# Implicit-filter taps computed with time on the partitions, their norm and the bias term summed by accumulating DMAs, and the convolution's output rows formed one quarter later

## The chip, the cores and the metric

The kernel runs on one core of a Trainium2 chip. The metric is the device time of one execution in microseconds, the median of several runs; one further execution was recorded by the profiler. Everything is float32; products of large matrices are made as three matmuls of a high and a low part (hi x hi, hi x lo, lo x hi).

## The reference

One encoder layer on 512 tokens of width 2048. An RMS-normalised input is projected; two branches run on it, a Hyena branch (gated long convolution, 1024 channels) and grouped-query attention; they are gated, merged and projected, and a SwiGLU feed-forward network follows. The change touches the Hyena branch alone:

```python
def implicit_filter(L, w1, b1, w2, b2, w3, b3, w4, freq):
    ...                                  # z: 33 features of each of the 512 positions
    h = jnp.sin(fr * (z @ w1 + b1))
    h = jnp.sin(fr * (h @ w2 + b2))
    h = jnp.sin(fr * (h @ w3 + b3))
    h = h @ w4                           # (512, 2048): a forward and a backward filter per channel
    ...
    decay = jnp.exp(-t[:, None] * deltas[None, :])
    h_fwd = h[:, :HYENA_W] * decay
    h_bwd = h[:, HYENA_W:] * decay
    k = jnp.concatenate([h_fwd, jnp.zeros((1, HYENA_W), f32), h_bwd[:0:-1]], axis=0)
    return k / jnp.sum(jnp.abs(k), axis=0, keepdims=True)

    x0, x1, hv = jnp.split(u_h, HYENA_ORDER + 1, axis=-1)     # after a 3-tap convolution
    z = hv * x1
    z = bidir_fft_conv(z, filt) + hy_bias * z
    y_h = z * x0
```

So the taps are made by a small network from the positions, damped, divided by the sum of their absolute values, and convolved with z through a transform of 1024 points; a bias times z is added.

## The kernel before

The 1024 Hyena channels are handled in four quarters q of 256 channels, each two tiles c of 128 channels. The main program (the loop over q near line 602) multiplies the 16 input tiles xg by weight blocks of 128 x 128 (`group`: three matmuls per block), makes x1, hv and x0 with `short_conv`, and then z and its even and odd parts zf. Weights come in tiles of 1024 columns: a load on SP's queue into one of two buffers, a cast on ScalarE (wh) and a subtraction on VectorE (wl), each with three buffers.

The filter work is woven into this stream. Generators stand in one queue (`side`); after every weight block `step()` counts one step, and when the number that a generator yielded has passed, its next part is emitted. The order of TensorE is exactly that of emission; the other engines' orders are made by a scheduler with priorities, and stay in order on the chip. The queue holds `mlp_gen` (the three sine layers, once), `taps_gen(0)`, a pause, `filter_gen(0)`, and then for each q `conv_gen(q)`, which contains `taps_gen(q + 1)`, and `filter_gen(q + 1)`.

- `taps_gen(q)` multiplies the last layer's output (hh, hl: 64 hidden units twice on the partitions, 512 positions along the row) by w4: channels on the partitions, time along the row (fp). VectorE multiplies by the decay (dec), giving fd and bd; ScalarE sums the absolute values along the row (scr), VectorE makes 1/norm (rn), adds norm times bias into tap zero, and folds the two halves into hs and hd.
- `filter_gen(q)` turns hs and hd by 16 transposes on TensorE (ktp), so that time is on the partitions, twists them (kt, with priority), splits them into high and low parts (k..h, k..l), and after TURN_WAIT steps transforms them (kp). The spectrum (G, then K) is written to a DRAM tile kd by POOL.
- `conv_gen(q)` transposes and transforms zf (ztp, up), loads the spectrum in two halves fb (kc, POOL's queue), multiplies (cu, cv, Y), and after Y_WAIT steps transforms back (ab); ab times rn gives abs, whose sums and differences are y, and y times x0 is yh.

PSUM has eight banks in one rotation; the tag tmp has five buffers of 128 x 512, the tag wk seven. After the last quarter the key/value projection (kv) runs, `flush()` emits what is left of the queue, and the memory of this stage is released to attention. The q, attention, gate and feed-forward stages that follow are not changed.

Of the kernel before, what the change touches and what calls it, by code (L numbers as in the profile page):

```python
# [40 lines left out]
RS_STEP = 8  # L41
TURN_WAIT = 8, 8, 10, 11
Y_WAIT = 11, 13, 11, 15
# [74 lines left out]

def layer_kernel(tc, wpk, xT, par, flt, zemb, w4, decT, tb2, rope, qkg, out):
    nc = tc.nc  # L120
# [189 lines left out]
    def mlp_gen():  # L310
# [15 lines left out]
        for l in range(3):  # L326
            csl = slice(l * P, (l + 1) * P)
            nk, nh = (P, 64) if l else (66, 33)
            hp = ps_tile(f"hp{l}")
            mm(hp, wh[:nk, csl], st[:nk], True, False)  # L330
            mm(hp, wl[:nh, csl], st[:nh], False, True)
            a = tmp(f"ha{l}")
            nn = tmp(f"hn{l}")
            nc.vector.tensor_scalar(a, hp, fl[:, 256 + l:257 + l], fl[:, 259:260], ALU.add, ALU.mult)
            nc.vector.tensor_scalar(nn, a, float(np.float32(1 / (2 * math.pi))), MAGIC, ALU.mult, ALU.add)
            nc.vector.tensor_scalar(nn, nn, MAGIC, None, ALU.subtract)
            for c in (C1, C2, C3):
                nc.vector.scalar_tensor_tensor(a, nn, -c, a, ALU.mult, ALU.add)
            nc.vector.tensor_scalar(a, a, PI32, -PI32, ALU.min, ALU.max)
            if l < 2:  # L340
                st = tpool.tile([P, S], F32R, tag="tmp", bufs=5, name=f"hs{l}")
                nc.scalar.activation(st, a, AF.Sin)
                casts["sin", l] = nc.scalar.activation(a[64:], a[64:], AF.Sin).ins
                nc.gpsimd.tensor_tensor(st[64:], a[64:], st[64:].bitcast(F32), ALU.subtract)
            else:
                nc.scalar.activation(a, a, AF.Sin)
                hh, hl = cw("hh", [P, S], "hh", dt=F32R), cw("hl", [P, S], "hl", dt=F32R)
                nc.scalar.copy(hh, a)
                nc.vector.tensor_tensor(hl, a, hh.bitcast(F32), ALU.subtract)
                mlp["h"] = hh, hl  # L350
            yield MLP_WAITS[l + 1]
            if l == 2:
                w4_parts(0)
                yield 6

    filt, kd, folded = {}, {}, {}
    w4t = {}
# [6 lines left out]
    def w4_parts(q):  # L364
# [5 lines left out]
        w4t[q] = w4s  # L370

    def taps_gen(q):

        w4s = w4t.pop(q)
        rn, hs_l, hd_l = [], [], []
        for c in range(2):
            dec = cw(f"dec{q}{c}", [P, S], "dec", 1)
            nc.scalar.dma_start(dec, decT[2 * q + c])
            fd = work(f"fd{q}{c}")
            bd = cw(f"bd{q}{c}", [P, S + 1], "bd", 1)  # L380
            for half, dst in ((0, fd), (1, bd[:, :S])):
                fp = ps_tile(f"fp{q}{c}{half}")
                csl = slice(half * 256 + c * P, half * 256 + (c + 1) * P)
                mm(fp, w4s[:, csl], mlp["h"][0], True, False)
                mm(fp, w4s[:, csl], mlp["h"][1], False, True)
                nc.vector.tensor_tensor(dst, fp, dec, ALU.mult)
                yield 2
            nc.vector.memset(bd[:, S:S + 1], 0.0)
            n2 = cw(f"n2{q}{c}", [P, 2], "n2", 3)
            scr = tmp(f"scr{q}{c}")  # L390
            nc.scalar.activation(scr, fd, AF.Abs, accum_out=n2[:, 0:1])
            nc.scalar.activation(scr, bd[:, 1:], AF.Abs, accum_out=n2[:, 1:2])
            r = cw(f"rn{q}{c}", [P, 1], "rn", 4)
            nc.vector.tensor_tensor(r, n2[:, 0:1], n2[:, 1:2], ALU.add)
            nc.vector.scalar_tensor_tensor(fd[:, :1], r, pcol("hyb", 2 * q + c), fd[:, :1], ALU.mult, ALU.add)
            nc.vector.tensor_scalar(r, r, 256.0, None, ALU.mult)
            nc.vector.reciprocal(r, r)
            rn.append(r)

            hs, hd = work(f"hs{q}{c}"), work(f"hd{q}{c}")  # L400
            ahead = fd.rearrange("p (m n) -> p n m", n=2)
            back = bd[:, 1:].rearrange("p (m n) -> p n m", n=2)[:, ::-1]
            for h, op in ((hs, ALU.add), (hd, ALU.subtract)):
                h = h.rearrange("p (n m) -> p n m", n=2)
                nc.vector.tensor_tensor(h[:, :, :P], ahead[:, :, :P], back[:, :, :P], op)
                nc.vector.tensor_tensor(h[:, :, P:][:, :, ::-1], ahead[:, :, P:], back[:, :, P:], op)
            hs_l.append(hs)
            hd_l.append(hd)
        folded[q] = rn, hs_l, hd_l

    def filter_gen(q):
        rn, hs_l, hd_l = folded.pop(q)
        if q + 1 < NQ:
            w4_load(q + 1)
        yield 3
        taps = []
        for i, src in enumerate((hs_l, hd_l)):
            tps = [ps_tile(f"ktp{q}{i}{j}") for j in range(2)]
            for j, tp in enumerate(tps):
                for n in range(4):  # L420
                    o = n // 2 * 256 + j * P
                    transpose(tp[:, n * P:(n + 1) * P], src[n % 2][:, o:o + P])
            with tc.high_priority():
# [6 lines left out]
        if q + 1 < NQ:  # L430
            w4_parts(q + 1)
        yield TURN_WAIT[q]

# [12 lines left out]
        for fb in range(2):  # L446
# [15 lines left out]
            yield 2  # L462
        filt[q] = rn

    zst, x0st, yh = {}, {}, [None] * HT

    def conv_gen(q):

        rn = filt[q]
        while q not in zst or side["n"] < zst[q][2]:  # L470
            yield 1
        zl, zf_l, _ = zst[q]
        zT = []
# [7 lines left out]
        ys = {}  # L481
        for fb in range(2):
            kc = []
            for ph in range(2):
# [9 lines left out]
            for ph in range(2):  # L494
# [9 lines left out]
                ys[ph, fb] = split(r3, y, "r", "r", 16, 16, f"Yt{q}{fb}{ph}")  # L504
                yield 5
        if q + 1 < NQ:
            yield from taps_gen(q + 1)
        yield Y_WAIT[q]
        abs_ = [work(f"abs{2 * q + c}") for c in range(2)]
        for ph in range(2):  # L510
            ab = [ps_tile(f"ab{q}{ph}{c}") for c in range(2)]
            for fb in range(2):
                yhi, ylo = ys[ph, fb]
                a = fb * 256
                for low in range(2):
                    for c in range(2):
                        for i in range(2):
                            csl = slice(i * 256 + c * P, i * 256 + (c + 1) * P)
                            o = ab[c][:, i * 256:(i + 1) * 256]
                            if low:  # L520
                                mm(o[:, :P], ylo[:, csl], part(i, 0, a, a + P), False, fb == 1 and i == 1, skip_group_check=True)
                            else:
                                both = CS[i].rearrange("p (h t) -> p h t", h=2)[:, :, a:a + P]
                                mm(o, yhi[:, csl], both, fb == 0 and i == 0, False, skip_group_check=True)
            yield 4
            for c in range(2):
                low = tmp(f"abl{q}{ph}{c}")[:, :256].rearrange("p (i t) -> p i t", i=2)
                src = ab[c].rearrange("p (i h t) -> p i h t", i=2, h=2)
                nc.scalar.activation(low, src[:, :, 1], AF.Copy, scale=rn[c])
                dst = abs_[c].rearrange("p (i s t) -> p i s t", i=2, s=2)[:, :, ph]  # L530
                nc.vector.scalar_tensor_tensor(dst, src[:, :, 0], rn[c], low, ALU.mult, ALU.add)
        yield 1
        for c in range(2):
            ct = 2 * q + c
# [4 lines left out]
            nc.vector.tensor_tensor(down[:, :, ::-1], a, b, ALU.subtract)  # L539
            while ct not in x0st:  # L540
                yield 1
            yh[ct] = x0st[ct]
            nc.vector.tensor_tensor(yh[ct], yh[ct], y, ALU.mult)


    xps = [ps_tile(f"px{i}") for i in range(XW)]
    xg, acc1 = [], work("acc1")
# [54 lines left out]
    for q in range(NQ):  # L602
        zl, zf_l = [], []
        for c in range(2):
# [10 lines left out]
            hv = short_conv(p2, 16 + ct, f"hv{ct}", cw(f"hvo{ct}", [P, S], "sc", 3))  # L615
            z = cw(f"z{ct}", [P, S], "z", 3)
            nc.vector.tensor_tensor(z, hv, x1, ALU.mult)
            zf = cw(f"zf{ct}", [P, S], "sc", 3)
            after, ahead = (z[:, h * 256:(h + 1) * 256].rearrange("p (t s) -> p s t", s=2) for h in (1, 0))
            for i, op in enumerate((ALU.add, ALU.subtract)):  # L620
                nc.vector.tensor_tensor(zf[:, i * 256:(i + 1) * 256].rearrange("p (s t) -> p s t", s=2),
                                        after, ahead[:, :, ::-1], op)
            zl.append(z)
            zf_l.append(zf)
# [791 lines left out]
def _constants():  # L1416
# [22 lines left out]
    ang = (f4(2.0 * math.pi) * pos / f4(S))[:, None] * fb[None, :]  # L1439
    zemb = two_part(np.ascontiguousarray(np.concatenate([t[:, None], np.cos(ang), -np.sin(ang)], axis=-1).T, dtype=f4)).reshape(66, S)  # L1440
    lo_d, hi_d = math.log(1e-2) / 1.5, math.log(1e-2) / 0.3
    deltas = np.abs(np.linspace(lo_d, hi_d, HW, dtype=f4))
    dec = np.exp(-t[:, None] * deltas[None, :]).astype(f4)
    decT = dec.T.reshape(HT, P, S)

# [3 lines left out]
    for half, pp in ((0, tok // 64), (1, tok % 64)):  # L1449
# [3 lines left out]
        for j, v in enumerate((np.concatenate([c, c], 1), np.concatenate([-s, s], 1))):  # L1453
            rope[:, j, :, b:b + 64] = v.reshape(NTB, P, 64).transpose(1, 0, 2)
    return tb2, cosw, sinw, cosa, sina, zemb, decT, rope


def _arrays(inp):
    f4 = np.float32
    a = {k: np.asarray(v)[0] for k, v in inp.items()}  # L1460
    assert all(v.dtype == f4 for v in a.values())
    tb2, cosw, sinw, cosa, sina, zemb, decT, rope = _constants()

# [43 lines left out]
    xT = a["x"].T.reshape(KT, P, S)  # L1507
    arr = dict(wpk=wpk, xT=xT, par=par, flt=flt, zemb=zemb, w4=w4, decT=decT, tb2=tb2, rope=rope, qkg=qkg)
    return {k: np.ascontiguousarray(v, dtype=f4) for k, v in arr.items()}
# [15 lines left out]
```

## Time and profile before

| | us |
|---|---|
| median of 3 runs | 2494.44 (2492.99 to 2495.07) |
| the profiled execution | 2493.58 |
| its span in the profile | 2491.8 |

TensorE (PE) is busy in all of the span, VectorE (DVE) in 84%, ScalarE (ACT) in 48%, GpSimd (POOL) in 7%. The granted clock of TensorE is full throughout. In the rows of the profile that follow, a timeline row reads: start, busy time, engine, line, operation, result <- inputs, shapes, count, and in brackets the idle time before it and what ended it; a row of waits reads: who, for whom, total, times, longest; a row of stretches reads: stretch and length, then busy us and instruction count of PE, PEld (weight loads), DVE, ACT and POOL, the clock, the DMA engines' share and GB/s. Names like wl or kt are the program's tiles.

### The profile page before, as it was taken

To read this page: it belongs to the slowest core of one execution; us is meant where nothing else is said; L and a number is where in the kernel's file an instruction comes from. 1 tells how busy PE (TensorE), PEld (TensorE's weight loads), DVE (VectorE), ACT (ScalarE), POOL (GpSimd) and SP (SyncE) were. 2 spreads that over 40 slices of the span, in tenths; PEclk is the share of its full clock that TensorE was granted. 3 is DMA by queue.
4 is the path that set the end of the run, shared out by engine and by line. 5 is a ranking of instruction groups with operands and counts; after the bars stand their busy time and mean duration, and the time that the engine had idled before them with its cause. 6 is when DMAs were issued, how large, how long until landed. Compare 5 with 4: busy or idle time off the path is not lost.

```text
span 2491.8 us, 34447 instructions
## 1 busy us (share of the span) xinstructions
PE 2485.5 (100%) x13114; PEld 2140.8 (86%) x13114; DVE 2089.3 (84%) x2972; ACT 1191.4 (48%) x1778; POOL 185.0 (7%) x297
## 2 busy tenths in 40 slices
PE   9999999999999999999999999999999999999999
PEld 7888888888888888888888888888888888888888
DVE  8899986764589999555999989999999988998888
ACT  6444334654554455443544444444444455445443
POOL 0000113020000000000000000000000002001111
PEclk9999999999999999999999999999999999999999
DMA  6434443233554444644333333333333348557754
GB/s 216 132 123 131 140 144 113 70 102 119 185 177 157 148 141 152 194 163 136 121 125 117 127 117 120 127 120 127 118 119 125 121 144 221 146 146 187 193 152 110
DMA packets 113571, 350.48 MB, mean 141 GB/s; under 512 B 13987, under 2 KB 15267, under 8 KB 113181
## 3 DMA queue, kind: packets, MB, share of 16 engines
q1 hardware_dynamic: 70128, 248.02, 30.2%
q0 software_dynamic: 22832, 63.19, 9.6%
q10 hardware_dynamic: 20445, 37.07, 4.9%
q8 instruction: 103, 1.69, 0.3%
q14 instruction: 63, 0.52, 0.1%
HBM read 297.63 MB, written 54.26 MB: 141 GB/s over the span
## 4 chain that ended last, share of the span: by engine, by line
PE 96%; DVE 2%; DMA 1%; issue 0%; ACT 0%; ACTq 0%; SPq 0%; DVEq 0%; POOLq 0%
PE fx L137 19%; PE fy L137 10%; PE b L137 7%; PE o L137 7%; PE gx L137 7%; PE px L137 6%; PE d L137 5%; PE fz L137 5%; PE dx L137 4%; PE q L137 4%; PE ex L137 3%; PE gy L137 3%; PE phv L137 2%; PE ey L137 2%; PE dy L137 2%; PE kv L137 2%
## 5 line engine op out<-in xcount | busy, mean ns | idle before, releaser
L195 DVE TENSOR_TENSOR wl<-wr,wh 128x1024 fp32r<-128x1024 f32 (+1 forms) x168 | 201.2, 1198 | 110.8 <-ACT wh L194 110.6
L194 ACT CAST wh<-wr 128x1024 fp32r<-128x1024 f32 (+1 forms) x168 | 173.3, 1032 | 236.6 <-PE o L137 67.1
L919 ACT CAST fwhs<-fs 128x1024 fp32r<-128x1024 f32 x176 | 184.8, 1050 | 88.7 <-PE fz L137 73.6
L921 DVE TENSOR_TENSOR fwls<-fs,fwhs 128x1024 fp32r<-128x1024 f32 x176 | 214.3, 1218 | 4.3 <-ACT fwhs L919 4.2
L919 ACT CAST fwha<-fa 128x1024 fp32r<-128x1024 f32 x132 | 139.0, 1054 | 149.4 <-PE fx L137 83.4
L137 PE MATMUL px<-xh,wh 128*128 128x512 f32 x576 | 179.4, 393 | 0.4 <-ACT xh L559 0.3
L137 PE MATMUL fy<-fX,fwhs 128*128 128x512 f32 x704 | 175.4, 391 | 0.0
L137 PE MATMUL fx<-fX,fwhs 128*128 128x512 f32 x704 | 175.2, 391 | 0.0
L137 PE MATMUL fx<-fX,fwha 128*128 128x512 f32 x704 | 171.8, 391 | 0.0
L921 DVE TENSOR_TENSOR fwla<-fa,fwha 128x1024 fp32r<-128x1024 f32 x132 | 161.3, 1222 | 10.0 <-ACT fwha L919 9.9
L137 PE MATMUL o<-ms,wh 128*128 128x512 f32 x512 | 157.7, 389 | 0.0
L137 PEld LDWEIGHTS fx<-fX,fwha 128*128 128x128 f32 x704 | 129.3, 188 | 25.0
L137 PEld LDWEIGHTS fx<-fX,fwhs 128*128 128x128 f32 x704 | 129.2, 188 | 25.1
L137 PEld LDWEIGHTS fy<-fX,fwhs 128*128 128x128 f32 x704 | 129.2, 188 | 24.9
L137 PEld LDWEIGHTS px<-xh,wh 128*128 128x128 f32 x576 | 106.7, 188 | 23.3 <-issue 0.7
L137 PE MATMUL d<-act,wh 128*128 128x512 f32 x384 | 118.2, 389 | 0.0
L137 PEld LDWEIGHTS o<-ms,wh 128*128 128x128 f32 x512 | 96.0, 188 | 19.8
L137 PE MATMUL px<-xh,wl 128*128 128x512 f32 x288 | 112.5, 391 | 0.0
L912 DVE TENSOR_TENSOR fs<-fa,fa 128x1024 f32<-128x1024 f32 x88 | 107.0, 1217 | 1.7 <-PE o L137 1.0
L912 DVE TENSOR_TENSOR fs<-fs,fa 128x1024 f32<-128x1024 f32 x88 | 107.2, 1218 | 0.9 <-PE o L137 0.2
L137 PE MATMUL o<-ms,wl 128*128 128x512 f32 x256 | 99.6, 389 | 0.0
L137 PE MATMUL fy<-fX,fwls 128*128 128x256 f32 x704 | 98.7, 283 | 0.2 <-DVE fwls L921 0.2
(979 smaller groups left out, 5883.0 us busy)
## 6 DMA issues: line engine op xcount, KB each, us to landing
fa<-wpk SPq DMA_DIRECT2D x176, 512.0 KB, 3.6
wr<-wpk SPq DMA_DIRECT2D x162, 512.0 KB, 3.5
ga<-wpk SPq DMA_DIRECT2D x60, 512.0 KB, 3.7
da<-wpk SPq DMA_DIRECT2D x32, 512.0 KB, 3.7
ea<-wpk SPq DMA_DIRECT2D x32, 512.0 KB, 4.4
actd<-c POOLq DMA_DIRECT2D x41, 256.0 KB, 4.2
actr<-actd ACTq DMA_DIRECT2D x41, 256.0 KB, 5.1
x2d<-dt POOLq DMA_DIRECT2D x32, 256.0 KB, 5.7
```

The costliest lines, as they stand in the source:

```text
L137: tc.keep_in_program_order(nc.tensor.matmul(out, lhsT=lhsT, rhs=rhs, start=start, stop=stop, **kw))
L194: casts[i] = nc.scalar.copy(st["hi"][:, c], st["raw"][:, c]).ins
L195: nc.vector.tensor_tensor(st["lo"][:, c], st["raw"][:, c], st["hi"][:, c].bitcast(F32), ALU.subtract)
L912: raws["sum"] = nc.vector.tensor_tensor(t, a, b, ALU.add).ins
L919: raws["wh"] = nc.scalar.copy(hi, w).ins
L921: raws["wl"] = nc.vector.tensor_tensor(lo, w, hi.bitcast(F32), ALU.subtract).ins
```

## The change

The features (zemb) are put into another order on the host, all even positions first, so that 128 columns of hh, taken from an offset, are just the positions that one transformed row block needs. In `taps_gen` hh and hl now stand as the stationary operand and w4 moves: fp comes out with time on the partitions and 256 channels along the row for each of two shifts, and the transposes in `filter_gen` are gone. hh and hl get two more columns, and the decay table (decP) is laid out anew, with a zero where the missing tap lies.

The sum over time now runs across partitions. The absolute values of the four tiles of a quarter (fa) are written to one DRAM tile by POOL's queue, the last three with addition in the DMA; `norm_load` brings the sum back on ScalarE's queue and adds its two halves on POOL, and `norm_taps` sums over partitions with two one-column matmuls and makes 1/norm. The bias no longer goes into tap zero: half of bias times zf is written to DRAM (zh, zd), and added to abs by a DMA with addition into SBUF; in the last quarter it is loaded (zr) and added on VectorE. The part that makes y and yh becomes `y_rows`, which for the first three quarters is emitted in the next quarter's `filter_gen`, ahead of TURN_WAIT. Buffers: two for dec instead of one, two for z instead of three, none for bd. TURN_WAIT of the last quarter goes from 11 to 10.

```diff
-TURN_WAIT = 8, 8, 10, 11
+TURN_WAIT = 8, 8, 10, 10
...
-                hh, hl = cw("hh", [P, S], "hh", dt=F32R), cw("hl", [P, S], "hl", dt=F32R)
-                nc.scalar.copy(hh, a)
-                nc.vector.tensor_tensor(hl, a, hh.bitcast(F32), ALU.subtract)
+                hh, hl = (cw(n, [P, S + 2], n, dt=F32R) for n in ("hh", "hl"))
+                for o, src in ((slice(0, 385), a[:, :385]), (slice(386, 513), a[:, 385:]),
+                               (slice(385, 514, P), a[:, P:P + 1].to_broadcast([P, 2]))):
+                    nc.scalar.copy(hh[:, o], src)
+                    nc.vector.tensor_tensor(hl[:, o], src, hh[:, o].bitcast(F32), ALU.subtract)
...
+    TAPS = ((0, 129), (386, 257)), ((1, 129), (385, 257))
+    norms, rns, sums = {}, {}, {}
     def taps_gen(q):
+        folded[q] = []
+        for j in range(2):
+            fb = []
+            for b in range(2):
+                dec = cw(f"dec{q}{j}{b}", [P, S], "dec", 2)
+                nc.scalar.dma_start(dec, decP[4 * q + 2 * j + b])
+                fp = ps_tile(f"fp{q}{j}{b}")
+                for n in range(2):
+                    a = TAPS[b][j][n]
+                    for i in range(2):
+                        mm(fp[:, n * 256:(n + 1) * 256], mlp["h"][i][:, a:a + P], w4s[:, b * 256:(b + 1) * 256],
+                           n == 0 and i == 0, n == 1 and i == 1, skip_group_check=True)
+                f = work(f"f{q}{j}{b}")
+                nc.vector.tensor_tensor(f, fp, dec, ALU.mult)
+                t = tmp(f"fa{q}{j}{b}")
+                nc.scalar.activation(t, f, AF.Abs)
+                if j + b:
+                    nc.gpsimd.dma_start(norms[q], t, accum_op=ALU.add)
+                else:
+                    norms[q] = dpool.tile([P, S], F32, tag=f"nd{q}", bufs=1, name=f"nd{q}")
+                    nc.gpsimd.dma_start(norms[q], t)
+                fb.append(f)
+                if not b:
+                    yield 2
+            f, b = fb
+            hs = work(f"hs{q}{j}")
+            nc.vector.tensor_tensor(hs, f, b, ALU.add)
+            nc.vector.tensor_tensor(f, f, b, ALU.subtract)
+            folded[q].append((hs, f))
+            yield 2
+
+    def norm_load(q):
+        t = tmp(f"na{q}")
+        nc.scalar.dma_start(t, norms[q])
+        norms[q] = cw(f"fo{q}", [P, 256], "fo", 1)
+        nc.gpsimd.tensor_tensor(norms[q], t[:, :256], t[:, 256:], ALU.add)
+
+    def norm_taps(q):
+        acc = norms.pop(q)
+        nr = ps_tile(f"nr{q}")
+        for c in range(2):
+            mm(nr[:, c:c + 1], acc[:, c * P:(c + 1) * P], pcol("one"), True, True)
+        r = cw(f"rn{q}", [P, 2], "rn", 2)
+        nc.vector.tensor_scalar(r, nr[:, :2], 256.0, None, ALU.mult)
+        nc.vector.reciprocal(r, r)
+        rns[q] = [r[:, c:c + 1] for c in range(2)]
...
     def filter_gen(q):
-        for i, src in enumerate((hs_l, hd_l)):
-            tps = [ps_tile(f"ktp{q}{i}{j}") for j in range(2)]
-            for j, tp in enumerate(tps):
-                for n in range(4):
-                    o = n // 2 * 256 + j * P
-                    transpose(tp[:, n * P:(n + 1) * P], src[n % 2][:, o:o + P])
+        for i, tps in enumerate(zip(*folded.pop(q))):
...
         if q + 1 < NQ:
             w4_parts(q + 1)
+        if q:
+            y_rows(q - 1, sums.pop(q - 1))
         yield TURN_WAIT[q]
...
     def conv_gen(q):
         for fb in range(2):
+            if fb:
+                norm_load(q)
...
+        norm_taps(q)
         if q + 1 < NQ:
             yield from taps_gen(q + 1)
         yield Y_WAIT[q]
...
+            if ph and q == NQ - 1:
+                zr = [tmp(f"zr{c}") for c in range(2)]
+                for c in range(2):
+                    nc.scalar.dma_start(zr[c], zd[c])
             yield 4
+            rn = rns[q]
...
+        if q < NQ - 1:
+            for c in range(2):
+                nc.gpsimd.dma_start(abs_[c], zd[c], accum_op=ALU.add)
+            yield 1
+            sums[q] = abs_
+            return
         yield 1
+        for c in range(2):
+            nc.vector.tensor_tensor(abs_[c], abs_[c], zr[c], ALU.add)
+        y_rows(q, abs_)
+
+    def y_rows(q, abs_):
...
-            while ct not in x0st:
-                yield 1
             yh[ct] = x0st[ct]
...
+    hybh = cw("hybh", [P, HT], "hybh")
+    nc.vector.tensor_scalar(hybh, prm[:, PC["hyb"]:PC["hyb"] + HT], 0.5, None, ALU.mult)
...
-            z = cw(f"z{ct}", [P, S], "z", 3)
+            z = cw(f"z{ct}", [P, S], "z", 2)
...
-            zl.append(z)
+            zl.append(dpool.tile([P, S], F32, tag=f"zd{ct}", bufs=1, name=f"zd{ct}"))
+            zh = tmp(f"zh{ct}")
+            nc.scalar.activation(zh, zf, AF.Copy, scale=hybh[:, ct:ct + 1])
+            nc.gpsimd.dma_start(zl[c], zh)
```

More of the change, by code (lines that the diff above doesn't have):

```diff
@@ L116, in weight_blocks, with layer_kernel @@
     return out
-def layer_kernel(tc, wpk, xT, par, flt, zemb, w4, decT, tb2, rope, qkg, out):
+def layer_kernel(tc, wpk, xT, par, flt, zemb, w4, decP, tb2, rope, qkg, out):
     nc = tc.nc
@@ L354, in mlp_gen @@
                 yield 6
-    filt, kd, folded = {}, {}, {}
+    kd, folded = {}, {}
     w4t = {}
@@ L370, in w4_parts @@
         w4t[q] = w4s
+    TAPS = ((0, 129), (386, 257)), ((1, 129), (385, 257))
+    norms, rns, sums = {}, {}, {}
     def taps_gen(q):
         w4s = w4t.pop(q)
-        rn, hs_l, hd_l = [], [], []
-        for c in range(2):
[L377 to L408, printed above, removed]
@@ L409, in taps_gen @@
-        folded[q] = rn, hs_l, hd_l
+        folded[q] = []
[28 more added lines that the diff above has]
+            yield 2
@@ L411, in filter_gen @@
     def filter_gen(q):
-        rn, hs_l, hd_l = folded.pop(q)
         if q + 1 < NQ:
@@ L462, in filter_gen @@
             yield 2
-        filt[q] = rn
     zst, x0st, yh = {}, {}, [None] * HT
     def conv_gen(q):
-        rn = filt[q]
         while q not in zst or side["n"] < zst[q][2]:
             yield 1
-        zl, zf_l, _ = zst[q]
+        zd, zf_l, _ = zst[q]
         zT = []
@@ L1439, in _constants @@
     ang = (f4(2.0 * math.pi) * pos / f4(S))[:, None] * fb[None, :]
-    zemb = two_part(np.ascontiguousarray(np.concatenate([t[:, None], np.cos(ang), -np.sin(ang)], axis=-1).T, dtype=f4)).reshape(66, S)
+    zemb = two_part(np.ascontiguousarray(np.concatenate([t[:, None], np.cos(ang), -np.sin(ang)], axis=-1).T, dtype=f4))
+    order = np.concatenate([i[:257:2], i[1:256:2], i[511:256:-2], i[510:257:-2]])
+    zemb = zemb.reshape(66, S)[:, order]
     lo_d, hi_d = math.log(1e-2) / 1.5, math.log(1e-2) / 0.3
@@ L1443, in _constants @@
     dec = np.exp(-t[:, None] * deltas[None, :]).astype(f4)
-    decT = dec.T.reshape(HT, P, S)
+    p = i[:P]
+    n = np.arange(2)[:, None]
+    at = np.stack([[2 * p + n, 2 * p + 2 - n], [510 - 2 * p + n, 512 - 2 * p - n]])
+    decP = np.concatenate([dec, np.zeros((1, HW), f4)])[at].reshape(4, 2, P, NQ, 256)
+    decP = decP.transpose(3, 0, 2, 1, 4).reshape(4 * NQ, P, S)
     inv = np.power(f4(10000.0), -np.arange(0, 64, 2, dtype=f4) / f4(64)).astype(f4)
@@ L1454, in _constants @@
             rope[:, j, :, b:b + 64] = v.reshape(NTB, P, 64).transpose(1, 0, 2)
-    return tb2, cosw, sinw, cosa, sina, zemb, decT, rope
+    return tb2, cosw, sinw, cosa, sina, zemb, decP, rope
 def _arrays(inp):
@@ L1461, in _arrays @@
     assert all(v.dtype == f4 for v in a.values())
-    tb2, cosw, sinw, cosa, sina, zemb, decT, rope = _constants()
+    tb2, cosw, sinw, cosa, sina, zemb, decP, rope = _constants()
     blocks = weight_blocks()
@@ L1507, in _arrays @@
     xT = a["x"].T.reshape(KT, P, S)
-    arr = dict(wpk=wpk, xT=xT, par=par, flt=flt, zemb=zemb, w4=w4, decT=decT, tb2=tb2, rope=rope, qkg=qkg)
+    arr = dict(wpk=wpk, xT=xT, par=par, flt=flt, zemb=zemb, w4=w4, decP=decP, tb2=tb2, rope=rope, qkg=qkg)
     return {k: np.ascontiguousarray(v, dtype=f4) for k, v in arr.items()}
```

## The prediction

> **What bounds the kernel now.** I read the page's first lines, then who waited for whom on TensorE, then the busy time by stretches, then TensorE's own timeline in the filter stage (roughly 44 to 372 us, where all the changed code runs).
>
> ```profile
> span 2491.8 us, 34447 instructions
> PE 2485.5 (100%) x13114; PEld 2140.8 (86%) x13114; DVE 2089.3 (84%) x2972; ACT 1191.4 (48%) x1778; POOL 185.0 (7%) x297
> ```
>
> ```profile
> PE warm L137 <- DVE wones L252: 1.1, 1, 1.1
> PE kp L137 <- DVE k121l L216: 0.5, 1, 0.5
> PE px L137 <- ACT xh L559: 0.3, 1, 0.3
> PE fy L137 <- DVE fwls L921: 0.2, 1, 0.2
> ```
>
> ```profile
> 200.00:260.00 60.00, 59.52 (x289) 49.61 (x288) 58.60 (x98) 29.59 (x47) 3.13 (x6) 1.00 0.37 115
> ```
>
> TensorE waits about 2 us in the whole program. "Busy" alone proves little, since matmul ends are modelled, but the four waits are the complete list, and the timeline below shows matmuls starting at a constant pitch. So the time is a sum of TensorE pitches; taking work off another engine earns nothing, and anything that makes TensorE wait costs in full. In the third row VectorE (58.60 of 60 us, the third pair) is almost as full: the second bound, close behind.
>
> The profiled execution took 2493.58 us (span 2491.8); the median of the runs is 2494.44, 0.86 higher. I work the change in us against the profiled execution and add it to the median.
>
> **Part 1: the tap transposes leave TensorE.** Eight blocks of eight 128x128 transposes (ktp) go.
>
> ```profile
> 88.38 0.39 PE L137 MATMUL px<-xh,wl 128*128 128x512 f32 x1
> 88.61 0.62 PE L137 MATMUL phv<-xh,wh 128*128 128x512 f32 x2
> 89.06 0.39 PE L137 MATMUL phv<-xh,wl 128*128 128x512 f32 x1
> 89.29 1.03 PE L140 MATMUL ktp<-ident,hs 128*128 128x128 f32 x8
> ...
> 90.86 0.39 PE L137 MATMUL phv<-xh,wh 128*128 128x512 f32 x1
> ```
>
> One weight block is three matmuls, 0.68 us from wl to wl (88.38 to 89.06), a pitch of 0.227. From 88.61 to 90.86 stand two such triples and one transpose block: 2.25 - 1.36 = 0.89 us, with its bubble behind it. Eight blocks: **-7.1 us**.
>
> **Part 2: the tap matmuls turn around.** Before, each of 16 filter tiles had two 512-column matmuls; now each has four of 256 columns, with four weight loads.
>
> ```profile
> 132.97 0.61 PE L137 MATMUL px<-xh,wh 128*128 128x512 f32 x2
> 133.65 0.39 PE L137 MATMUL fp<-hh,w4s 128*128 128x512 f32 x1
> ...
> 134.81 0.39 PE L137 MATMUL px<-xh,wh 128*128 128x512 f32 x1
> ...
> 1201.04 1.12 PE L137 MATMUL fz<-fX,fwla 128*128 128x256 f32 x8
> 1201.99 2.00 PE L137 MATMUL fx<-fX,fwha 128*128 128x512 f32 x8
> ```
>
> Old block: 134.81 - 132.97 - 1.36 = 0.48. The matmuls of 256 columns run at 0.95 / 8 = 0.119, four make 0.475, and about 0.02 of changing over remains: 0.50. Difference 0.02 x 16 = **+0.3 us**. Low end 0. High end: a block that mixes 256 and 128 columns (ab, below) takes 150.78 - 148.26 - 0.68 = 1.84, against 0.95 for its eight long and 0.8 for its eight short ones: a bubble of 0.09, so +1.4.
>
> ```profile
> 148.26 0.39 PE L137 MATMUL px<-xh,wl 128*128 128x512 f32 x1
> ...
> 150.78 0.40 PE L137 MATMUL px<-xh,wl 128*128 128x512 f32 x1
> ```
>
> **Part 3: the norm matmuls come.** norm_taps adds two one-column matmuls per quarter. The nearest row is the same operation in token_rstd, four such matmuls that show as eight.
>
> ```profile
> 56.98 0.62 PE L137 MATMUL px<-xh,wh 128*128 128x512 f32 x2
> 57.67 0.95 PE L137 MATMUL rs1ss<-prm,acc 128*128 128x1 f32 x8
> 59.26 0.39 PE L137 MATMUL px<-xh,wh 128*128 128x512 f32 x1
> ```
>
> 59.26 - 56.98 - 1.36 = 0.92 for eight. Four of them: 0.4 for the pitch and 0.1 for the bubble, 0.5 a quarter, **+2.0 us**. Ends: half a block, 1.8; a full block each, 3.7.
>
> **Part 4: one wait that should go.**
>
> ```profile
> 250.39 0.40 PE L137 MATMUL kp<-k121h,CS 128*128 128x512 f32 x1
> 251.26 0.49 PE L137 MATMUL kp<-k121l,CS 128*128 128x512 f32 x1 [0.47 <-DVE k121l L216]
> ```
>
> ```profile
> 233.69 0.42 DVE L406 TENSOR_TENSOR hd<-fd,bd 128x256 f32<-128x256 f32 x1
> 240.50 0.75 DVE L427 SCALAR_TENSOR_TENSOR kt<-ktp,prm,kt 128x512 f32<-128x512 f32 x1
> 250.52 0.69 DVE L216 TENSOR_TENSOR k121l<-kt,k121h 128x512 fp32r<-128x512 f32 x1
> ```
>
> The matmul at 251.26 started 0.87 after its neighbour instead of 0.23, 0.64 lost, because k121l was late. Its chain begins with kt at 240.50, although the folded taps were ready at 234.1: the 6 us between were spent on the transposes' turn. Without them, and with y of the quarter before emitted after the taps instead of ahead of them, the chain starts earlier. TensorE arrives about 2 us earlier (two blocks of 0.89), less than the 6. I take **-0.6 us**; the other end is 0. TURN_WAIT of the last quarter, one step less, moves the same matmuls by 0.68 us in TensorE's order, costs nothing while that chain is early, and up to 0.68 if it isn't.
>
> **Part 5: what lies beside TensorE.** Per quarter VectorE loses eight half-width folds and eight single-column operations and gains four full-width folds and two small ones; at the end two adds of zr come.
>
> ```profile
> L406 DVE TENSOR_TENSOR hd<-fd,bd x8: 411/418/422, 83.2 to 306.2; 128x256 f32<-128x256 f32 x8
> L617 DVE TENSOR_TENSOR z<-hvo,x1o 128x512 f32<-128x512 f32 x8 | 5.5, 685 | 0.1
> ```
>
> Folds: 32 x 0.42 = 13.4 out, 16 x 0.69 = 11.0 in; zr 1.4 in; with the small ones VectorE comes out slightly lighter. ScalarE gains eight zh (about 0.62 each, as the 128x512 cast quoted under rival 2, 5 us in 328) and loses the accumulator reads; it is half idle in the third row. The hh and hl pieces and hybh, under a microsecond together, lie ahead of the first fp. POOL and the DMA engines gain 16 norm writes (12 adding), four norm loads, eight zd writes, six adding loads, two zr loads and eight more dec loads: 44 x 256 KB = 11 MB in 328 us, 34 GB/s beside the 115 of the row above. All of that is hidden by the lead with which weights are ready:
>
> ```profile
> 142.38 1.05 ACT L194 CAST wh<-wr 128x1024 fp32r<-128x1024 f32 x1 [2.15 <-PE px L137]
> ```
>
> ```profile
> 145.43 1.22 DVE L195 TENSOR_TENSOR wl<-wr,wh 128x1024 fp32r<-128x1024 f32 x1
> ```
>
> The cast at 142.38 starts when TensorE frees one of three buffers, so its tile is needed two tiles, 48 x 0.227 = 10.9 us, later, at 153.3 at the earliest. wl ends at 146.65: 6.6 us of cover. A VectorE or ScalarE delay below that costs nothing; above it, every microsecond counts. The y rows and the sum of the bias move behind the adding load; y is read only after the kv matmuls, so lateness there is free unless VectorE stands waiting for it.
>
> **The sum:** -7.1 + 0.3 + 2.0 - 0.6 = **-5.4 us**: 2493.58 becomes 2488.2, the median **2489.0**. By the ends of the terms: -7.1 + 1.8 - 0.64 = -5.9 to -7.1 + 1.4 + 3.7 = -2.0. About 0.2% (5.0 us) is what a measurement of this kernel can tell from no change, so the sum stands just outside it.
>
> **Rival 1, slower: the adding DMAs hold the buffers.** The four norm writes of a quarter go to one DRAM tile, so each must wait for the one before; each holds one of the five tmp buffers until it lands, and POOL stands behind it.
>
> ```profile
> kd<-K POOLq DMA_DIRECT2D x24, 256.0 KB, 3.3
> x2d<-dt POOLq DMA_DIRECT2D x32, 256.0 KB, 5.7
> ...
> POOL out L1373 <- DMA x2d<-dc: 30.7, 14, 4.7
> ```
>
> The third row shows POOL standing 2.2 us on average, 4.7 at most, for an adding DMA whose result the next one reads. The chain: 3.3 + 3 x 5.7 = 20.4 us. [...] The rows below show the first and the last of the second quarter's four filter tiles read out of PSUM 6.5 us apart; their absolute values follow, so the buffers stay held about 20.4 - 7 = 13 us beyond the last; in that time short_conv's u, abl and kt want them, and VectorE runs in order, wl behind u. If that stops it for the whole 13, 6.6 are covered and 6.8 are TensorE's, in four quarters 27: 2494.4 + 27 - 5.4 = 2516. It decides from 2.6 us a quarter (10.4 in all), a stop of 9.2. For it: the third row of the first part, VectorE has 1.4 us in 60 to catch up. Against it: one buffer in five stays free, and each landing frees another.
>
> ```profile
> 147.76 0.68 DVE L386 TENSOR_TENSOR bd<-fp,dec 128x512 f32<-128x512 f32 x1
> ...
> 154.25 0.68 DVE L386 TENSOR_TENSOR bd<-fp,dec 128x512 f32<-128x512 f32 x1
> ```
>
> **Rival 2, no change: TensorE waits for the norm.** The norm matmul stands in TensorE's fixed order 10 steps and one up block (10 x 0.68 + 1.4 = 8 us) behind norm_load. It needs a load by ScalarE's queue and an add on POOL.
>
> ```profile
> dec<-decT ACTq DMA_DIRECT2D x8, 256.0 KB, 2.9
> ...
> 381.35 4.38 POOL L675 TENSOR_TENSOR rpk<-rpk,gaink 128x128 f32<-128x128 f32 x8 [26.95 <-DVE kss L687]
> ```
>
> ```profile
> 132.54 0.62 ACT L215 CAST Yt001h<-Y 128x512 fp32r<-128x512 f32 x1 [1.95 <-DVE Y L503]
> ```
>
> 2.9 + 2 x 0.55 = 4 us fit into 8. But if the issue stands behind the cast at 132.54, the norm comes at 137 where TensorE (fp at 133.65) wants it: 3.5 us lost a quarter. Half of that, 7 us, gives 2494.4 - 5.4 + 7 = 2496; the whole gives 2503.
>
> **Rival 3, the change does not do what it says:** VectorE, not TensorE, paces the filter stage, and what leaves TensorE is spent on waiting for wl: 2494. For it the 58.60 of 60; against it the 6.6 us of lead and the four waits.
>
> **How the numbers follow.** The sum arrives, with no new wait above a microsecond: 0.66; its ends (-5.9 to -2.0) lie mostly near -5.4, so 0.42 of it beyond -0.2% and 0.24 within. Rival 1: 0.16 (0.14 slower, 0.02 within). Rival 2: 0.12 (0.09 within, 0.03 slower). Rival 3: 0.06, within. Together 0.42 faster, 0.41 the same, 0.17 slower. The forecast's own range is 2487.5 to 2492.5; the range for 8 in 10 goes from 2487.0, half a microsecond below the best sum, to 2500, which takes in most of rival 2 and the weak half of rival 1.
>
> **What would show it.**
>
> ```profile
> 371.89 0.40 PE L137 MATMUL q<-wh,xh 128*128 128x512 f32 x1
> ```
>
> Right: no ktp rows; fp four at a time at about 0.12 pitch, nr of four at 0.4 to 0.5; TensorE's waits still at 1 to 3 us in all, without kp; the first q matmul starts at 366 to 367 us, where it stood at 371.9 before. Wrong by rival 1: TensorE waiting for wl or wh in the filter stage, and behind it VectorE or ScalarE waiting for DMA rows of the norm tile; by rival 2: TensorE rows "nr" that wait for POOL's add; by rival 3: no transposes, yet the q matmuls start where they did. The forecast falls if TensorE's waits in the filter stage exceed 5 us, whichever engine ends them.

## The result and the profile after

| | before | after |
|---|---|---|
| median, us | 2494.07 | 2530.89 (2527.19 to 2535.57) |
| the profiled execution, us | 2493.58 | 2535.57 |
| its span | 2491.8 | 2533.8 |

The ratio is 1.0149, 95% interval 1.0135 to 1.0164: 37 us slower, where 5 us faster was forecast.

The page's first lines, the changed kernel:

```profile
span 2533.8 us, 34488 instructions
PE 2497.9 (99%) x13098; PEld 2147.1 (85%) x13098; DVE 2089.0 (82%) x2929; ACT 1196.4 (47%) x1772; POOL 211.6 (8%) x331
```

VectorE's busy time is what it was (2089.3 before), ScalarE's is 5 us more (1191.4 before), GpSimd's 27 (185.0 before), on an engine that is idle for 92% of the span. No added work accounts for 37 us; engines waited. Who waited for whom on TensorE (the largest rows of 18):

```profile
PE nr L137 <- POOL fo L416: 8.9, 2, 5.0
PE px L137 <- DVE rn L425: 5.0, 1, 5.0
PE fp L137 <- DVE cv L513: 4.5, 1, 4.5
PE kp L137 <- DVE k111l L216: 2.4, 1, 2.4
```

All rows together make 32 us, against 2 before. The weights' wl and wh are in none of them. The filter's own tiles are late: the norm, the taps k, the products cu and cv. The rest is in the stretches (length, busy time of PE, PEld, DVE, ACT, POOL, then the granted clock):

```profile
100.00:150.00 50.00, 43.33 (x183) 34.70 (x184) 37.72 (x53) 17.88 (x25) 8.90 (x14) 0.91 0.49 154
```

The clock is 0.91 here, and 1.00 in such rows of before. TensorE's timeline behind one of the waits shows it:

```profile
159.12 1.19 PE L137 MATMUL px<-xh,wh 128*128 128x512 f32 x2 [5.05 <-DVE rn L425]
160.11 0.63 PE L137 MATMUL px<-xh,wl 128*128 128x512 f32 x1
...
161.39 0.63 PE L137 MATMUL px<-xh,wl 128*128 128x512 f32 x1
...
165.90 0.40 PE L137 MATMUL px<-xh,wl 128*128 128x512 f32 x1
...
166.59 0.40 PE L137 MATMUL px<-xh,wl 128*128 128x512 f32 x1
```

From wl to wl a triple takes 1.28 us (160.11 to 161.39) and not 0.69 (165.90 to 166.59) for some 5 us after the wait.

Behind the late tiles stand rows for which the kernel before has no counterpart (the first 560 us, other engines; nd is the norm's DRAM tile, fa the absolute values):

```profile
POOL nd L397 <- DMA nd<-fa: 26.2, 5, 5.7
ACT abl L549 <- DMA nd<-fa: 14.3, 5, 4.0
ACT kt L438 <- DMA nd<-fa: 7.4, 4, 3.5
```

The first quarter's four norm writes on POOL's timeline, and what stood behind them on VectorE and ScalarE:

```profile
82.72 0.54 POOL L400 DMA_DIRECT2D nd<-fa  x1
88.58 0.90 POOL L397 DMA_DIRECT2D nd<-fa  x1 [5.31 <-DMA nd<-fa]
93.81 0.88 POOL L397 DMA_DIRECT2D nd<-fa  x1 [4.33 <-DMA nd<-fa]
98.55 0.86 POOL L397 DMA_DIRECT2D nd<-fa  x1 [3.87 <-issue]
```

```profile
88.15 0.69 DVE L627 TENSOR_TENSOR x01u<-px,rbc 128x512 f32<-128x512 f32 x1 [2.39 <-DMA nd<-fa]
...
93.36 0.69 DVE L627 TENSOR_TENSOR x12u<-px,rbc 128x512 f32<-128x512 f32 x1 [2.72 <-DMA nd<-fa]
```

```profile
98.07 0.72 ACT L438 ACTIVATE kt<-hs,prm 128x512 f32<-128x512 f32 x1 [2.04 <-DMA nd<-fa]
...
102.80 0.73 ACT L438 ACTIVATE kt<-f,prm 128x512 f32<-128x512 f32 x1 [0.99 <-DMA nd<-fa]
```

Each write goes out when the one before has landed (the fourth write's row names no releaser, but kt on ScalarE was let go by a landing at 98.07, half a us ahead of it); the last lets its tmp buffer go at 102.8, 20.1 us after the first. x01u, x12u and kt read nothing of the norm; they wait for a tmp buffer that a write still holds. This is rival 1.

The second thing is on ScalarE's timeline; after, and then before:

```profile
120.69 0.72 ACT L657 ACTIVATE zh<-zf,hybh 128x512 f32<-128x512 f32 x1
121.31 0.57 ACT L455 COPY kc<-kp 128x512 f32<-128x512 f32 x1
```

```profile
105.01 0.59 ACT L441 COPY kc<-kp 128x512 f32<-128x512 f32 x1 [1.28 <-PE kp L137]
```

The second copy of the first quarter's spectrum runs 16 us later than before, right behind zh. zh takes one of the five tmp buffers and is emitted ahead of that copy, and its input zf is made late; the copy, which takes the next buffer, comes behind it.

### The profile page after: what moved, and what is told of

It is laid out like the page before. It is cut to its first block, busy times and chain, and to the rows that moved or that the text cites. A ratio compares the mean times of both kernels' runs of the same rounds, so it can differ in the third digit from the quotient of the medians.

```text
span 2533.8 us, 34488 instructions
## 1 busy us (share of the span) xinstructions
PE 2497.9 (99%) x13098; PEld 2147.1 (85%) x13098; DVE 2089.0 (82%) x2929; ACT 1196.4 (47%) x1772; POOL 211.6 (8%) x331
## 4 chain that ended last, share of the span: by engine, by line
PE 83%; DVE 2%; DMA 1%; issue 0%; ACT 0%; POOL 0%; DVEq 0%; ACTq 0%; POOLq 0%
PE fx L137 19%; PE fy L137 9%; PE b L137 7%; PE o L137 7%; PE gx L137 7%; PE fz L137 5%; PE d L137 5%; PE q L137 3%; PE ex L137 3%; PE dx L137 3%; PE gy L137 3%; PE ey L137 2%; PE dy L137 2%; PE gz L137 2%; PE kv L137 1%; PE dz L137 1%
## 5 line engine op out<-in xcount | busy, mean ns | idle before, releaser
L137 PEld LDWEIGHTS o<-ms,wh 128*128 128x128 f32 x512 | 96.0, 188 | 20.1
```

The costliest lines, as they stand in the source:

```text
L137: tc.keep_in_program_order(nc.tensor.matmul(out, lhsT=lhsT, rhs=rhs, start=start, stop=stop, **kw))
```

## The experiments

The theories, in the order in which they came up: (1) the serial chain of adding writes holds tmp buffers; (2) TensorE meets the norm's matmuls too early in its order; (3) the bias term's extra traffic costs; (4) the norm's result nr holds a PSUM bank; (5) zh's tmp buffer delays the spectrum. Of these 1 and 5 stood; a part of 3 stays open. Each ratio is to runs of the kernel before that were taken with it.

**The norm summed without DMAs.** Seven adds of 256 columns by GpSimd in SBUF for each quarter (one for the first filter tile, two for each of the others); no norm DMA, no norm_load.

```diff
-                    nc.gpsimd.dma_start(norms[q], t, accum_op=ALU.add)
+                    for h in range(2):
+                        nc.gpsimd.tensor_tensor(norms[q], norms[q], t[:, h * 256:(h + 1) * 256], ALU.add)
                 else:
-                    norms[q] = dpool.tile([P, S], F32, tag=f"nd{q}", bufs=1, name=f"nd{q}")
-                    nc.gpsimd.dma_start(norms[q], t)
+                    norms[q] = cw(f"fo{q}", [P, 256], "fo", 1)
+                    nc.gpsimd.tensor_tensor(norms[q], t[:, :256], t[:, 256:], ALU.add)
...
-            if fb:
-                norm_load(q)
```

> The changed kernel, but the four tiles of absolute values of a quarter are summed in SBUF by adds on GpSimd (eight 128x256 adds a quarter) instead of by four serial DMAs and a load. Theory T1 (each adding DMA of a quarter waits for the one before, some 5 to 6 us, and meanwhile its tmp buffer is held, so VectorE and ScalarE stop in order): nearly all of the loss goes, 2490 to 2502 us, and the waits of VectorE and ScalarE for the norm tile's DMAs are gone. T2 (the loss is the norm that comes late to the nr matmuls in TensorE's fixed order, and the lower clock behind it): the norm is early here too, so the nr waits go, 9 us and as much again for the clock, but the kp and up waits stay: about 2513. T3 (the bias path costs it): about 2525.

Measured: 2508.87, ratio to before 1.0063 (1.0048 to 1.0078): 22 of the 37 us come back. TensorE's three large waits now are px for rn 5.0, px for cv 4.9, fp for cv 3.7; the spectrum's second copy still starts at 115.69, behind zh. That is less than theory 1 had (2490 to 2502). The norm's DMAs are the larger cause and not the only one.

**The norm's matmuls later in TensorE's order**, behind taps_gen of the next quarter.

```diff
-        norm_taps(q)
         if q + 1 < NQ:
             yield from taps_gen(q + 1)
+        norm_taps(q)
```

> The changed kernel, with the two norm matmuls of a quarter emitted behind the next quarter's taps (8 steps, some 6 us later in TensorE's order), all DMAs as they are. T1: only the 9 us of nr waits and a part of the bank waits behind them can go, the holding of buffers stays: 2518 to 2531. T2: most of the loss goes, 2495 to 2510. T3: about 2525 to 2531.

Measured: 2531.19, ratio 1.0154 (1.0137 to 1.0171): nothing gained. The wait for fo is gone, and px for rn rose to 6.8, nr for cv to 5.9: TensorE waits for the same backlog at other places. That nr waited was a symptom; theory 2 falls.

**The bias term left out.**

```diff
-            zh = tmp(f"zh{ct}")
-            nc.scalar.activation(zh, zf, AF.Copy, scale=hybh[:, ct:ct + 1])
-            nc.gpsimd.dma_start(zl[c], zh)
...
-                nc.gpsimd.dma_start(abs_[c], zd[c], accum_op=ALU.add)
```

> The changed kernel without the bias term: no zh, no write to zd, no adding load into abs, no zr (the term is left out of the result); y is still made in the next quarter. T1: eight writes that hold tmp and stand ahead of the norm on POOL's queue go, a smaller share: 2515 to 2528. T2: 2525 to 2531. T3: back to 2490 to 2500.

Measured: 2519.42, ratio 1.0104 (1.0088 to 1.0119), 11.5 us less than the changed kernel. The norm's rows stay, and abl waits longer for them (23.0 us in 7 waits, 14.3 in 5 with the bias). Theory 3 alone would have had 2490 to 2500.

**The chain alone, in the kernel before.** The absolute values that it makes anyway get a tmp buffer each (before, two share one) and are also written to one DRAM tile, three of four adding; nothing reads it.

```diff
-            scr = tmp(f"scr{q}{c}")
...
+                scr = tmp(f"scr{q}{c}{i}")
...
+                if c + i:
+                    nc.gpsimd.dma_start(nd[q], scr, accum_op=ALU.add)
+                else:
+                    nd[q] = dpool.tile([P, S], F32, tag=f"nd{q}", bufs=1, name=f"nd{q}")
+                    nc.gpsimd.dma_start(nd[q], scr)
```

> The kernel before, with only the norm chain added: its four tiles of absolute values of each quarter, which it computes anyway, get a tmp buffer each and are written to one DRAM tile, the last three with addition; nothing reads them. T1: slower by 10 to 30 us, with waits for these DMAs on VectorE and ScalarE. T2 and T3: within 3 us of 2494, as nothing waits for the sum and the bias is untouched.

Measured: 2516.71, ratio 1.0091 (1.0076 to 1.0106). The waits of the other engines in the first 560 us:

```profile
POOL nd L394 <- DMA nd<-scr: 22.0, 6, 5.1
ACT abl L534 <- DMA nd<-scr: 20.1, 6, 4.0
ACT kt L431 <- DMA nd<-scr: 8.9, 3, 3.4
```

The changed kernel's rows, in a kernel that has nothing else of the change: 23 us (0.0091 x 2494), as much as taking the chain away gave back.

**The same writes, none adding.** Four DRAM tiles instead of one.

```diff
-                    nc.gpsimd.dma_start(nd[q], scr, accum_op=ALU.add)
+                nd[q, c, i] = dpool.tile([P, S], F32, tag=f"nd{q}{c}{i}", bufs=1, name=f"nd{q}{c}{i}")
+                nc.gpsimd.dma_start(nd[q, c, i], scr)
```

> The kernel before, with the four absolute-value tiles of each quarter written to four separate DRAM tiles by plain DMAs, none adding; nothing reads them. It differs from the kernel before with the chain of adding DMAs (2516.7) only in that no write has to wait for another. Theory 1 (the adds are serial, and hold the tmp buffers): each write lands in about 3.3 us by itself, the buffers come free as the tiles are made, so no wait of ACT abl or ACT kt for a DMA row of more than 1 us in all, TensorE waits below 4 us, 2494 to 2498. Rival: the four extra buffers taken and the 4 MB written are what costs, whatever the order of the writes: 2508 to 2517 with abl waiting for the norm's writes as with the chain. Third theory: POOL's issuing of the writes delays kd and kc: kd writes stand behind them by more than 2 us, 2498 to 2505.

Measured: 2495.99, ratio 1.0008 (0.9999 to 1.0017).

```profile
ACT abl L531 <- DMA nd<-scr: 4.2, 5, 2.1
ACT kt L428 <- DMA nd<-scr: 2.8, 1, 2.8
```

Same buffers, same bytes, same queue: the chain of adds costs about 21 of the 23 us, and not the buffers taken or the bytes. The two rows were expected below 1 us and make 7.0, but the time hardly shows them. One thing is not told apart: an add also takes longer to land (a median of 4.2 us over the chain's sixteen writes, twelve of them adding, against 3.4 here), and adds to four separate tiles were not run.

**The norm's matmuls alone, in the kernel before**, on stand-in data in a bank of their own, at the place that norm_taps has.

```diff
+        nr = ps_tile(f"nr{q}")
+        for c in range(2):
+            mm(nr[:, c:c + 1], ident, pcol("one"), True, True)
+        r = cw(f"nrr{q}", [P, 2], "nrr", 2)
+        nc.vector.tensor_scalar(r, nr[:, :2], 256.0, None, ALU.mult)
```

> The kernel before, with only a stand-in for the norm matmuls: at the place of norm_taps two one-column matmuls of the identity into a PSUM bank of their own, and one small VectorE operation that reads it; the result is not used. Theory T4 (the nr bank is a ninth where all eight are taken, and its reader stands far back in VectorE's order, so TensorE waits for it): slower by 8 to 20 us, with TensorE waits that end with this small operation or with cv. Rival (only the matmuls' own time counts): 2 us slower, no new waits.

Measured: ratio 1.0022 (1.0013 to 1.0031), 5.5 us, with one new wait, px for cv, 1.2 us. Of this, 2.0 us are the matmuls' own time by part 3; what the rest is was not taken apart, and it is less than the 8 to 20 us that theory 4 had.

**The norm's matmuls earlier**, in filter_gen ahead of TURN_WAIT, on top of the norm summed without DMAs.

```diff
+        norm_taps(q)
         yield TURN_WAIT[q]
...
-        norm_taps(q)
         if q + 1 < NQ:
```

> The kernel of e1_norm_pool (norm summed in SBUF by GpSimd), with the norm matmuls moved from conv_gen to filter_gen, behind the taps and ahead of TURN_WAIT, where the transposes' four banks used to stand. T4: the waits for rn go, and a part of those for cv: 2509 to 2494 to 2500. T5 (zh takes its tmp buffer ahead of the copy kc of the first quarter, which then stands behind zh in ScalarE's order, so the spectrum and with it all of the first conv_gen comes 11 us late): little change, 2503 to 2509, waits for cv stay.

Measured: 2510.52, ratio 1.0068 (1.0055 to 1.0081). No gain; the waits for rn became ab for cv 3.4, ab for f 2.5, kp for k030l 4.1.

**zh written over z**, on top of the last one, so that it takes no tmp buffer.

```diff
-            zh = tmp(f"zh{ct}")
+            zh = z
```

> The kernel of e6_norm_early, with zh written over z (which nothing reads any more) instead of into a tmp buffer. T4 alone: as e6. T5: the copy kc of the first quarter is back at 105 us, the first spectrum is written at 108 to 113 as before, and the waits for cv are gone. T4 and T5 together, as the sum of TensorE's own work has it: 2487 to 2492, some 3 to 6 us below the kernel before.

Measured: 2495.47, ratio 1.0007 (0.9998 to 1.0015), 15 us less from that one line, and still 3.5 above the range of the two theories together. The second spectrum copy is back where it was:

```profile
104.13 0.59 ACT L457 COPY kc<-kp 128x512 f32<-128x512 f32 x1 [1.26 <-PE kp L137]
```

TensorE's waits fell from 32 us to one beside the warm-up's:

```profile
PE up L137 <- DVE zt20l L216: 3.8, 1, 3.8
PE warm L137 <- DVE wones L252: 1.1, 1, 1.1
```

**The same line alone, the norm's DMAs kept.**

> The changed kernel as it is, with zh written over z instead of into a tmp buffer; the adding DMAs of the norm and the nr matmuls stay. T5: 5 to 12 us faster than the changed kernel (2519 to 2526), about what leaving the bias out gave. If the bias path costs by its DMAs (POOL's queue) and not by the buffer: unchanged, 2528 to 2533.

Measured: 2527.44, ratio 1.0135 (1.0122 to 1.0148): only 3.5 us less than the changed kernel, with intervals that overlap. That misses theory 5's range (2519 to 2526) and lies beside that of its rival. abl waits 22.6 us in 7 waits for nd rows there, kt 13.6 in 4 (14.3 and 7.4 in the changed kernel). Five buffers serve both, and while the chain holds them, one user less only moves the wait. The two causes do not add up as separate terms: zh's buffer is worth some 3.5 us beside the chain and 15 without it. Leaving the bias out gave 11.5 beside the chain, so about 8 us of the bias path are not zh's buffer there; which part of the path they are is not shown.

**More steps ahead of the up matmuls of the third quarter**, against the one wait left: 11 steps instead of 8, and 14.

```diff
-        yield 8
+        yield 11 if q == 2 else 8
```

> The changed kernel with the norm summed by GpSimd's adds in SBUF, the norm's matmuls moved to the filter's generator, zh written over z (2495.5 together), and in the third quarter alone 11 steps instead of 8 between the transposes of z and the first up matmuls. Left over there was one wait of TensorE, up for zt20l, 3.8 us, with about 4 us of slower matmuls behind it. Three steps are 2.0 us of other matmuls, so 1.8 us of the wait should be left if nothing else moves. Theory 6 (that wait and its slow stretch are all that the sum of TensorE's matmuls lacks): 2490 to 2493 here. Rival: VectorE is so full there that the wait only moves to the next tile behind it (u, v or wl): 2494 to 2497.

> The same with 14 steps: six more are 4.1 us of other matmuls, more than the 3.8 us of the wait. Theory 6: no TensorE wait above 1.5 us, first q matmul at 365 to 366, granted clock 1.00 throughout, 2486 to 2489, which would be the sum of the prediction's parts 1 to 3 with nothing lost. Rival (VectorE paces the third quarter): the wait returns at another tile, 2493 to 2498, and the taps or the kc loads of the last quarter come too late.

Measured: 2498.91, ratio 1.0019 (1.0010 to 1.0027), and 2504.87, ratio 1.0041 (1.0028 to 1.0055). Both slower than with 8. The wait shrank to 2.0 and to 0.4 us as worked out, and others came: 1.7, 1.1 and 1.0 us at f, zt30l and x17u with 11 steps, 4.6 us at f and 2.8 at Yt311h with 14. That one wait was all that stood between this version and a gain: this theory (6) falls. VectorE's timeline says why: the first product of the third quarter, before, and then with 11 steps:

```profile
271.80 1.23 DVE L498 TENSOR_TENSOR cu<-up,kc 128x1024 f32<-128x1024 f32 x1 [3.02 <-DMA kc<-kd]
```

```profile
273.99 1.22 DVE L512 TENSOR_TENSOR cu<-up,kc 128x1024 f32<-128x1024 f32 x1 [5.31 <-DMA kc<-kd]
```

TensorE stood about 4 us ahead of before by then (below), and this product comes 2 us later than before: the spectrum reaches it by way of VectorE, DRAM and back, none of which was made shorter. Its first step on VectorE, G, starts at 252.45 and at 251.12 before, although TensorE finishes the matmuls ahead of it some 4 us earlier; the y rows stand there now.

**The y rows behind the spectra**, on top of zh over z, with 8 steps.

```diff
-        if q:
-            y_rows(q - 1, sums.pop(q - 1))
         norm_taps(q)
...
             yield 2
+        if q:
+            y_rows(q - 1, sums.pop(q - 1))
```

> The changed kernel with the norm summed by GpSimd's adds in SBUF, its matmuls in the filter's generator and zh over z (2495.5 together), and the y rows of the quarter before emitted behind the filter spectra instead of ahead of the norm's matmuls. In the third quarter the six y instructions (2.9 us) stood on VectorE just ahead of the first G, which started at 252.9 though the copy it reads ended at 250.2; the late G, K and zt20l made the one wait of TensorE that is left (3.8 us, and some 4 us of slower matmuls behind it). Theory 7 (order on VectorE, not its load): G 2.5 us earlier, zt20l ends at 262 and the wait at up shrinks below 1.5 us; 2487 to 2490.5, faster than before. Rival (VectorE's load paces the filter stage, as in rival 3 of the prediction: it carries 275 us of work in 60 to 360 here, 273 before): the y rows cost the same wherever they stand, and a wait of 2 us or more turns up behind their new place, at u, v, wl or the taps of the next quarter: 2493 to 2499.

Measured: 2506.94, ratio 1.0050 (1.0036 to 1.0063), slower than the version it was to mend by 11 us. The loss begins in the second quarter, where TensorE still reaches up as early (186.85, and 187.08 in that version). VectorE's timeline there, in that version and then with the y rows moved:

```profile
184.81 0.48 DVE L472 SCALAR_TENSOR_TENSOR K<-G,prm,kci 128x256 f32<-128x256 f32 x1
...
193.66 1.23 DVE L512 TENSOR_TENSOR cu<-up,kc 128x1024 f32<-128x1024 f32 x1 [1.49 <-DMA kc<-kd]
```

```profile
180.51 0.75 DVE L468 SCALAR_TENSOR_TENSOR K<-G,prm,kci 128x512 f32<-128x512 f32 x1 [2.00 <-DMA kd<-K]
...
189.52 0.48 DVE L470 SCALAR_TENSOR_TENSOR K<-G,prm,kci 128x256 f32<-128x256 f32 x1
...
198.38 1.23 DVE L512 TENSOR_TENSOR cu<-up,kc 128x1024 f32<-128x1024 f32 x1 [2.82 <-DMA kc<-kd]
```

K waits for an earlier K to have been written: the abs tiles live longer, and take two of the seven wk buffers from it. The last K and the first cu come 4.7 us later, and TensorE then waits 0.9 us for cu and 2.7 for f. In the third quarter it reaches up 5.9 us later (266.30), when zt20l is done (263.50): the wait at up is gone because TensorE is late, and not because the order helped. So this falls too (7), and its rival, that the six y instructions cost the same load wherever they stand, isn't what the row shows either: it is the buffer rotation once more.

## Why the prediction was wrong

**The step that failed is part 5**: "All of that is hidden by the lead with which weights are ready". The lead of 6.6 us was measured on wl and holds for wl: no wait for wl or wh shows in the filter stage after the change. It was applied to everything on VectorE and ScalarE, though k, zt, cu, cv and rn have leads of their own: in before, k121l had none at all (the 0.5 us wait of part 4). And the DMAs were counted in bytes, 34 GB/s, where what they cost is the time for which they hold a buffer: the chain alone, put into the kernel before, took 23 us, and the same bytes without it 2. Of the 42 us between the two profiled executions, with the 5.4 that the sum expected to gain, 30 are new waits of TensorE; about 17 more are the clock's, by the changed kernel's row for the whole stretch (0.05 x 340), and no term of the prediction has them:

```profile
60.00:400.00 340.00, 309.76 (x1391) 254.20 (x1390) 269.10 (x395) 131.88 (x188) 55.04 (x82) 0.95 0.53 151
```

**Parts 1 to 3 were right.** The page has no ktp. Two of the new blocks, the tap matmuls in the changed kernel and the norm's in the version at 2495.5:

```profile
139.62 0.40 PE L137 MATMUL px<-xh,wl 128*128 128x512 f32 x1
139.86 0.28 PE L137 MATMUL fp<-w4s,hh 128*128 128x256 f32 x1
...
140.79 0.39 PE L137 MATMUL px<-xh,wl 128*128 128x512 f32 x1
```

```profile
93.59 0.40 PE L137 MATMUL phv<-xh,wl 128*128 128x512 f32 x1
93.82 0.50 PE L137 MATMUL nr<-prm,fo 128*128 128x1 f32 x4
...
94.73 0.40 PE L137 MATMUL phv<-xh,wl 128*128 128x512 f32 x1
```

1.17 - 0.68 = 0.49 for fp (0.50 was taken), 1.14 - 0.68 = 0.46 for nr (0.5). **Part 4** holds once the buffers are free: no kp wait there, against 8.5 us in nine rows of the changed kernel. The first up matmul of the third quarter shows the parts together; before, and then in that version:

```profile
264.33 0.39 PE L137 MATMUL up<-zt20h,CS 128*128 128x512 f32 x1
...
272.53 0.39 PE L137 MATMUL up<-zt20h,CS 128*128 128x512 f32 x1
```

```profile
260.44 0.40 PE L137 MATMUL up<-zt20h,CS 128*128 128x512 f32 x1
264.66 0.80 PE L137 MATMUL up<-zt20l,CS 128*128 128x512 f32 x1 [3.82 <-DVE zt20l L216]
...
275.26 0.40 PE L137 MATMUL up<-zt20h,CS 128*128 128x512 f32 x1
```

TensorE is 3.89 us ahead there; three quarters of the terms (-5.3, +0.2, +1.5, -0.6) make -4.2. Then the one wait takes it all: from the first block of up to the second it is 14.82 us instead of 8.20, 6.6 lost on a wait of 3.8.

**Rival 1** had mechanism and place, and a chance of 0.16. Its chain of 20.4 us was 20.1, its 27 us were 23 measured alone, and both owe something to luck. In the chain the first, plain write took 5.9 us to the next issue, where 3.3 was priced, and the other three steps 5.2, 4.7 and 4.3, where 5.7 was. That each write waits for the one before was an assumption, and the rows of nd show it: POOL stood 5.31 and 4.33 us until the write before had landed. The 27 came by way of wl's 6.6 us of cover, but of TensorE's waits in that kernel only 1.5 us are for wh and wl, and most are for k and kt. What was set against it, "one buffer in five stays free, and each landing frees another", was the mistake: buffers go round in the order of emission, so the next user waits for its own buffer and not for any free one (VectorE was through with x00u at 85.76, and x01u waited on until 88.15), and an engine that runs in order stops with it. It was also too small: it foresaw one user of tmp, and zh, a second one, was priced as 0.62 us of ScalarE. Its sign ("TensorE waiting for wl or wh") named the wrong tiles for the changed kernel, for the same reason as part 5; the other half of it, VectorE and ScalarE waiting for DMA rows of the norm tile, is what the rows show. **Rival 2** showed as a row (nr for fo, 8.9 us) and was a symptom: taking the row away by moving nr gained nothing. **Rival 3**, 2494 at a chance of 0.06, is where the change lands without both holders: at 2495.5 TensorE's transposes are gone, its lead appears, and the stage doesn't end earlier (the first q matmul starts at 373.5, and at 371.9 before), because the filter's chain on VectorE and through DRAM is late there; the tile waited for is zt20l, and not wl as the rival had it. That is shown for the third quarter and the orders tried here; that no order would bring the 5 us home is not shown.

One end of the forecast's own range doesn't follow from its sum: 5.9 us below the median of 2494.44 is 2488.5, not 2487.5. Nothing above hangs on it.

## What to carry over

Before a transfer is called hidden, ask which buffer it holds, how long, and who is next in that rotation: bytes per second didn't say it here (the same bytes cost 23 us with the adds on one tile, and 2 without), and a chain of adding DMAs on one tile held its sources one after another (20 us for four, against a median of 3.4 each for plain writes). A lead is a property of one tile (6.6 us on wl, none on k121l); each tile that a change touches needs its own, measured to the matmul that reads it. A wait that moves when its reader is moved is a symptom (nr's 8.9 us for fo went when nr was moved, and 5.9 for cv came); look for the backlog behind it.

## What the runs showed of the hardware

In these runs a wait of TensorE could cost more than itself. Single waits of 2.0 us (zt20l with 11 steps), 1.7 (zt20l in the changed kernel) and 2.4 (k111l there) were followed by matmuls at their usual pitch; waits of 3.8 (the version at 2495.5), 3.9, 4.5 and 5.0 (the changed kernel) by matmuls at half speed (the granted clock was 0.50 from 159 to 162 us, behind the wait for rn), which lost another 2 to 3 us each. Short waits close together did the same: 2.0 and 1.0 us, at k030h and k030l of the changed kernel, and 0.7 and 0.9 us, at k101h and k101l, had half-speed matmuls behind them. The kernel with 11 steps shows the short kind:

```profile
264.23 0.50 PE L137 MATMUL up<-zt20l,CS 128*128 128x512 f32 x1 [1.99 <-DVE zt20l L216]
264.57 0.39 PE L137 MATMUL up<-zt20h,CS 128*128 128x512 f32 x1
264.80 0.39 PE L137 MATMUL up<-zt21h,CS 128*128 128x512 f32 x1
```

The pitch behind it is 0.23, where it is 0.43 behind the 3.8 us. But the length alone doesn't tell the two kinds apart. In the kernel with zh over z and the chain kept, a single wait as long has half-speed matmuls behind it, which begin 1.3 us after it:

```profile
313.75 0.38 PE L137 MATMUL fp<-w4s,hh 128*128 128x256 f32 x1 [2.04 <-DVE x17u L627]
...
314.79 0.40 PE L137 MATMUL phv<-xh,wl 128*128 128x512 f32 x1
...
315.84 0.63 PE L137 MATMUL phv<-xh,wl 128*128 128x512 f32 x1
...
317.12 0.63 PE L137 MATMUL phv<-xh,wl 128*128 128x512 f32 x1
```

Without the bias a single wait of 1.9 us (zt20l) did it too. In the filter stage every wait of 2.7 us or more that TensorE's timelines show was followed by half speed, and single ones of 1.9 to 2.5 us sometimes; what decides among those is not shown. Full speed came back 3 to 7 us after a single wait or after the first slow matmul. The prediction had charged a TensorE wait with its own length; for the waits of 3.8 to 5.0 us, 1.4 to 1.7 times that was nearer here.
